# A row softmax in hardware loops: four slots and semaphores that count down, for six slots and a written-out order

## The chip, the cores and the metric

The kernel runs on one core of a Trainium2 chip. The metric is the device time of one execution in microseconds (us), lower being better. Ten executions of the kernel before gave a median of 318.81 us, between 318.66 and 319.29.

Five engines of the core run their own instruction streams [...]. Of them this kernel uses the vector engine (DVE), the scalar engine (ACT) and the sync engine (SP), which here only issues transfers. Transfers between the main memory (HBM) and the on-chip memory are carried by 16 DMA engines. SP's transfers stand in one queue and ACT's in another.

## What is computed

```python
def setup_inputs():
    batch, seq, dim = 32, 512, 1024
    return {"x": np.random.randn(batch, seq, dim).astype(np.float32), "temperature": 0.5}

def reference(x, temperature):
    scaled = x / temperature
    shifted = scaled - np.max(scaled, axis=-1, keepdims=True)
    exp_x = np.exp(shifted)
    return (exp_x / np.sum(exp_x, axis=-1, keepdims=True)).astype(np.float32)
```

There are 32 x 512 = 16,384 rows of 1,024 fp32 numbers, 67.1 MB to be read and as much to be written. The temperature is a constant of the program.

## The kernel before

The rows are cut into 16 blocks of 1,024. Each of the 128 partitions takes 8 rows of a block, which lie behind one another in HBM, 32 KB in all. So a block is one load of 4 MB, 128 runs of 32 KB, and one store of the same shape. On chip the blocks stand in a ring of 48 rows a partition (`RING = 48`), that is six places of 8 rows, used in turn. A block is loaded into its place, changed there and stored from there.

The work on a block is done in two groups of four rows (`GROUP = 4`). For a group, DVE takes the maximum of its four rows in one instruction (`maximum`, L91) and multiplies the four maxima by minus the scale (`shift`, L101). ACT computes one exponential for each row, with that number as bias, and sums the row on the way (`exponential`, L109; the sum is fetched by a second instruction for each row, the READ_ACCUMULATOR). DVE inverts the four sums (`invert`, L122) and multiplies each row by its own (`divide`, L128).

All of it stands in one critical section, in which the framework adds no waits and keeps the order as written; the kernel has its own semaphores. Every semaphore only counts up, and each wait names the total it waits for (`topped` at g + 1 and so on), so that the wait is carried by the instruction that needs it. The three streams are:

- SP (L142): the 16 loads in order. The first six are issued at once; from then on load i waits until the store of block i - 6 has landed. At the end SP waits for the stores that are still out (L158).
- ACT: for each group g of 32 the four exponentials, and after the exponentials of the first group of block i + 1 the store of block i (`store`, L149), which waits until DVE has divided all of block i.
- DVE: the loop quoted here. The division of a group comes after the maximum of the next group, and so the last group of a block is divided after the first maximum of the next block, which waits for that block's load.

```python
        for g in range(len(groups) + 1):
            if g < len(groups):
                maximum(g)
                shift(g)
            if g > 0:
                invert(g - 1)
                divide(g - 1)
```

Everything is written out: there is no loop in the program that the chip runs.

Of the kernel before, what the change touches and what calls it, by code (L numbers as in the profile page):

```python
# [1 line left out]

# [4 lines left out]

LOADS = [8] * 16  # L10

STORES = [[8]] * 16

RING = 48

GROUP = 4


def _places(loads, ring):
    places, p = [], 0  # L20
    for k in loads:
        if p + k > ring:
            p = 0
        places.append(p)
        p += k
    return places


@with_exitstack
def kernel(  # L30
    ctx: ExitStack,
    tc: tile.TileContext,
    x: bass.AP,
    temperature: bass.AP,
    out: bass.AP,
):
    nc = tc.nc
    f32 = mybir.dt.float32
    scale = 1.0 / float(temperature)
    extreme = mybir.AluOpType.max if scale > 0 else mybir.AluOpType.min  # L40

    P = 128
    xf = x.flatten_outer_dims()
    of = out.flatten_outer_dims()
    n, d = xf.shape
    assert sum(LOADS) * P == n

    places = _places(LOADS, RING)
    first = [sum(LOADS[:i]) for i in range(len(LOADS))]
    total = sum(LOADS)  # L50

    pool = ctx.enter_context(tc.tile_pool(name="data", bufs=1))
    ring = pool.tile([P, RING, d], f32, name="ring")
    top = pool.tile([P, total], f32, name="top")
    bias = pool.tile([P, total], f32, name="bias")
    sums = pool.tile([P, total], f32, name="sums")
    recip = pool.tile([P, total], f32, name="recip")


    parts = []  # L60
    for i, ks in enumerate(STORES):
        j = 0
        for k in ks:
            parts.append((i, places[i] + j, first[i] + j, k))
            j += k
        assert j == LOADS[i]

    groups, part_end = [], []
    for i, s, r, k in parts:
        for a in range(0, k, GROUP):  # L70
            groups.append((i, s + a, r + a, min(GROUP, k - a)))
        part_end.append(len(groups))

    loaded = [tc.alloc_semaphore(f"loaded{i}") for i in range(len(LOADS))]
    stored = [tc.alloc_semaphore(f"stored{i}") for i in range(len(parts))]
    topped, biased, summed, inverted, scaled = (
        tc.alloc_semaphore(name)
        for name in ("topped", "biased", "summed", "inverted", "scaled")
    )

    def dram(t, r, k, i):

        block = t[P * first[i] : P * (first[i] + LOADS[i]), :]
        block = block.rearrange("(p k) d -> p k d", p=P, k=LOADS[i])
        return block[:, r - first[i] : r - first[i] + k, :]

    def maximum(g):
        i, s, r, k = groups[g]
        if g == 0 or groups[g - 1][0] != i:
            nc.vector.wait_ge(loaded[i], 16)  # L90
        nc.vector.tensor_reduce(  # L91
            out=top[:, r : r + k],
            in_=ring[:, s : s + k, :],
            axis=mybir.AxisListType.X,
            op=extreme,
        ).then_inc(topped, 1)

    def shift(g):
        i, s, r, k = groups[g]
        nc.vector.wait_ge(topped, g + 1)  # L100
        nc.vector.tensor_scalar_mul(  # L101
            bias[:, r : r + k], in0=top[:, r : r + k], scalar1=-scale
        ).then_inc(biased, 1)

    def exponential(g):
        i, s, r, k = groups[g]
        nc.scalar.wait_ge(biased, g + 1)
        for a in range(k):
            ins = nc.scalar.activation(  # L109
                ring[:, s + a, :],  # L110
                ring[:, s + a, :],
                mybir.ActivationFunctionType.Exp,
                bias=bias[:, r + a : r + a + 1],
                scale=scale,
                accum_out=sums[:, r + a : r + a + 1],
            )
        ins.then_inc(summed, 1)

    def invert(g):
        i, s, r, k = groups[g]  # L120
        nc.vector.wait_ge(summed, g + 1)
        nc.vector.reciprocal(recip[:, r : r + k], sums[:, r : r + k]).then_inc(inverted, 1)  # L122

    def divide(g):
        i, s, r, k = groups[g]
        nc.vector.wait_ge(inverted, g + 1)
        for a in range(k):
            ins = nc.vector.tensor_scalar_mul(  # L128
                ring[:, s + a, :], in0=ring[:, s + a, :], scalar1=recip[:, r + a : r + a + 1]
            )  # L130
        ins.then_inc(scaled, 1)

    def load(i):
        nonlocal free_to
        s, r, k = places[i], first[i], LOADS[i]

        for n, (l, s1, r1, k1) in enumerate(parts):
            if l < i and s1 < s + k and s < s1 + k1 and n > free_to:
                for b in range(free_to + 1, n + 1):
                    nc.sync.wait_ge(stored[b], 16)  # L140
                free_to = n
        nc.sync.dma_start(out=ring[:, s : s + k, :], in_=dram(xf, r, k, i)).then_inc(  # L142
            loaded[i], 16
        )

    def store(n):
        l, s, r, k = parts[n]
        nc.scalar.wait_ge(scaled, part_end[n])
        nc.scalar.dma_start(out=dram(of, r, k, l), in_=ring[:, s : s + k, :]).then_inc(  # L149
            stored[n], 16  # L150
        )

    free_to = -1
    with tc.tile_critical():  # L154
        for i in range(len(LOADS)):
            load(i)
        for b in range(free_to + 1, len(parts)):
            nc.sync.wait_ge(stored[b], 16)  # L158


        for g in range(len(groups) + 1):
            if g < len(groups):
                exponential(g)
            for n in range(len(parts)):
                if part_end[n] == g:
                    store(n)


        for g in range(len(groups) + 1):
            if g < len(groups):  # L170
                maximum(g)
                shift(g)
            if g > 0:
                invert(g - 1)
                divide(g - 1)


# [1 line left out]
_INS = ['x', 'temperature']  # L179
_OUTS = [((32, 512, 1024), 'float32')]  # L180

_NUMBERS = {'temperature': 0.5}


# [26 lines left out]
```

## Time and profile before

| | us |
|---|---|
| median of ten executions | 318.81 |
| the profiled execution, its own time | 319.1 |
| its span, from the first to the last instruction | 317.3 |
| one maximum of four rows on DVE (L91), mean | 4.414 |
| one division of a row on DVE (L128), mean | 0.749 |
| one exponential of a row on ACT (L109), mean | 1.137 |
| median from issue to landing, load | 51.3 |
| median from issue to landing, store | 38.0 |

The span is what all positions below refer to; 0 is its start. The execution's own time is 1.8 us longer than the span. Durations of neighbouring instructions on one engine overlap a little: a division takes 0.749 us by itself, but four in a row take 2.74. "Landing" is the moment when a transfer's semaphore has received its last count.

### The profile page before, as it was taken

The numbers are of one execution on the slowest core, as the hardware profiler recorded it, in microseconds if no ns is written. First come the engines' busy times: TensorE is split into PE (matmuls) and PEld (weight loads), VectorE is DVE, ScalarE is ACT, GpSimd is POOL, SyncE is SP. The second block draws the span as 40 slices with busy tenths as digits, with TensorE's granted clock in tenths as the row PEclk, the third lists the DMA queues.
The fourth block names the chain that finished last, engine by engine and source line by source line (L and its number), as shares of the span: only waits on it lengthen the run. The fifth ranks groups of instructions, "written<-read, shape, count | busy, mean of one in ns | idle before, by whom it ended". The sixth has DMA issues, their size and how long they took to land.

```text
span 317.3 us, 568 instructions
## 1 busy us (share of the span) xinstructions
DVE 235.4 (74%) x224; ACT 149.6 (47%) x257; POOL 0.2 (0%) x4
## 2 busy tenths in 40 slices
DVE  0399999999689494995949869496793967949710
ACT  1076666666526255361554606455163551635500
POOL 0000000000000000000000000000000000000000
DMA  8999999999999999999999999999999999999994
GB/s 322 405 463 401 397 459 434 425 452 409 454 405 459 405 454 421 438 454 405 459 401 463 401 459 421 435 450 409 459 405 455 409 450 430 430 446 413 459 405 207
DMA packets 4612, 134.25 MB, mean 423 GB/s; under 512 B 512, under 2 KB 512, under 8 KB 512
## 3 DMA queue, kind: packets, MB, share of 16 engines
q1 hardware_dynamic: 2304, 67.11, 49.4%
q10 hardware_dynamic: 2304, 67.11, 49.0%
q14 instruction: 4, 0.03, 0.0%
HBM read 67.11 MB, written 67.11 MB: 423 GB/s over the span
## 4 chain that ended last, share of the span: by engine, by line
DVE 72%; another core or an unknown queue 16%; DMA 4%; ACT 3%; issue 1%; SPq 0%
DVE top L91 43%; DVE ring L128 27%; DMA ring<-in_x_dram 4%; ACT ring L109 3%; DVE bias L101 2%; DVE recip L122 1%; SPq L206 0%; SPq L154 0%
## 5 line engine op out<-in xcount | busy, mean ns | idle before, releaser
L109 ACT ACTIVATE ring<-ring,bias 128x1024 f32<-128x1024 f32 x128 | 145.4, 1137 | 149.4 <-DVE bias L101 149.4
L91 DVE TENSOR_REDUCE top<-ring 128x4 f32<-128x4096 f32 x32 | 141.3, 4414 | 63.2 <-DMA ring<-in_x_dram 63.2
L128 DVE TENSOR_SCALAR ring<-ring,recip 128x1024 f32<-128x1024 f32 x128 | 87.7, 749 | 1.1
L109 ACT ACTIVATION_READ_ACCUMULATOR ring<-ring,bias 128x1 f32 x128 | 23.9, 187 | 0.0
L122 DVE RECIPROCAL recip<-sums 128x4 f32<-128x4 f32 x32 | 5.5, 171 | 2.0 <-ACT ring L109 2.0
L101 DVE TENSOR_SCALAR bias<-top 128x4 f32<-128x4 f32 x32 | 5.4, 169 | 1.1
L109 ACT ACT_TABLE_LOAD x1 | 1.3, 1283 | 0.9 <-SPq L154 0.9
L192 POOL MEMSET const-bfloat16-1.0<- 128x1 bf16 x1 | 0.1, 101 | 0.0
L192 POOL MEMSET const-uint8-127<- 128x1 uint8 x1 | 0.1, 101 | 0.0
L192 POOL MEMSET const-float32-0.0<- 128x1 f32 x1 | 0.1, 98 | 0.2 <-issue 0.2
L192 POOL MEMSET const-float32-1.0<- 128x1 f32 x1 | 0.1, 98 | 0.0
## 6 DMA issues: line engine op xcount, KB each, us to landing
ring<-in_x_dram SPq DMA_DIRECT2D x16, 4096.0 KB, 51.3
out_dram<-ring ACTq DMA_DIRECT2D x16, 4096.0 KB, 38.0
```

What stands on the lines that cost most here:

```text
L91: nc.vector.tensor_reduce(out=top[:, r : r + k], in_=ring[:, s : s + k, :], axis=mybir.AxisListType.X, op=extreme,).then_inc(topped, 1)
L101: nc.vector.tensor_scalar_mul(bias[:, r : r + k], in0=top[:, r : r + k], scalar1=-scale).then_inc(biased, 1)
L109: ins = nc.scalar.activation(ring[:, s + a, :], ring[:, s + a, :], mybir.ActivationFunctionType.Exp, bias=bias[:, r + a : r + a + 1], scal ...
L122: nc.vector.reciprocal(recip[:, r : r + k], sums[:, r : r + k]).then_inc(inverted, 1)
L128: ins = nc.vector.tensor_scalar_mul(ring[:, s + a, :], in0=ring[:, s + a, :], scalar1=recip[:, r + a : r + a + 1])
L192: nc = _bacc.Bacc("TRN2", target_bir_lowering=False, num_devices=1)
```

## The change

The ring has four slots of 8 rows a partition in place of six. The 16 blocks are done in four turns of four; block 4t + s uses slot s. Rows are assigned to blocks and partitions as before, and every transfer is still 4 MB in 128 runs of 32 KB.

DVE and ACT each run a hardware loop over the four turns (`Fori`), whose body holds the work of four blocks written out. A loop body is the same in each turn, so its waits can't name a growing total. In its place `take` is used: an instruction that waits until the semaphore has reached a count and then takes that count off. The semaphores of the loads and between the engines work in this way; `stored` still counts up, since its only waits are on SP, which has no loop.

On DVE the order within a block is now both maxima with their shifts, then both inversions and divisions; a block is finished before the next is begun. On ACT a block's store follows the exponentials of the same block. Its address in HBM is worked out from the loop's counter.

The last slot's final store is waited for in a second critical section.

```diff
-LOADS = [8] * 16
+SLOTS = 4
-STORES = [[8]] * 16
+ROWS = 8
-RING = 48
 GROUP = 4
...
+    xv = xf.rearrange("(t s p k) d -> s p t (k d)", s=SLOTS, p=P, k=ROWS)
+    ov = of.rearrange("(t s p k) d -> s p t (k d)", s=SLOTS, p=P, k=ROWS)
...
-    ring = pool.tile([P, RING, d], f32, name="ring")
-    top = pool.tile([P, total], f32, name="top")
+    ring = pool.tile([P, SLOTS, ROWS, d], f32, name="ring")
+    top = pool.tile([P, ROWS], f32, name="top")
...
+    def take(engine, sem, count=1):
+        engine.wait_ge(sem, count).then_inc(sem, -count)
...
+    def maximum(s, a):
         nc.vector.tensor_reduce(
+            out=top[:, a : a + GROUP],
+            in_=ring[:, s, a : a + GROUP, :],
             axis=mybir.AxisListType.X,
             op=extreme,
         ).then_inc(topped, 1)
-        nc.vector.wait_ge(topped, g + 1)
+        take(nc.vector, topped)
         nc.vector.tensor_scalar_mul(
...
+    def exponential(s, a):
+        take(nc.scalar, biased)
+        for r in range(a, a + GROUP):
...
+    def divide(s, a):
+        take(nc.vector, summed)
+        nc.vector.reciprocal(recip[:, a : a + GROUP], sums[:, a : a + GROUP]).then_inc(
+            inverted, 1
+        )
+        take(nc.vector, inverted)
+        for r in range(a, a + GROUP):
+            ins = nc.vector.tensor_scalar_mul(
+                ring[:, s, r, :], in0=ring[:, s, r, :], scalar1=recip[:, r : r + 1]
+            )
+        if a == starts[-1]:
+            ins.then_inc(scaled, 1)
...
+    with tc.tile_critical():
+        for t in range(turns):
+            for s in range(SLOTS):
+                if t > 0:
+                    nc.sync.wait_ge(stored[s], 16 * t)
+                nc.sync.dma_start(
+                    out=ring[:, s].rearrange("p k d -> p (k d)"), in_=xv[s][:, t, :]
+                ).then_inc(loaded[s], 16)
+        for s in range(SLOTS - 1):
+            nc.sync.wait_ge(stored[s], 16 * turns)
+        with nc.vector.Fori(0, turns):
+            for s in range(SLOTS):
+                take(nc.vector, loaded[s], 16)
+                for a in starts:
+                    maximum(s, a)
+                for a in starts:
+                    divide(s, a)
+        with nc.scalar.Fori(0, turns) as t:
+            for s in range(SLOTS):
+                for a in starts:
+                    exponential(s, a)
+                take(nc.scalar, scaled)
+                nc.scalar.dma_start(
+                    out=ov[s][:, bass.ds(t, 1), :],
+                    in_=ring[:, s].rearrange("p k d -> p (k d)").unsqueeze(1),
+                ).then_inc(stored[s], 16)
+    with tc.tile_critical():
+        nc.sync.wait_ge(
+            stored[-1], 16 * turns, synchronizes=[nc.sync.lower_ap(ring[:, SLOTS - 1])]
+        )
```

More of the change, by code (lines that the diff above doesn't have):

```diff
@@ L6 @@
 from concourse._compat import with_exitstack
-LOADS = [8] * 16
-STORES = [[8]] * 16
-RING = 48
+SLOTS = 4
+ROWS = 8
 GROUP = 4
[L19 to L26, printed above, removed]
 @with_exitstack
@@ L45 @@
     n, d = xf.shape
[L46 to L50, printed above, removed]
+    turns = n // (P * ROWS * SLOTS)
+    assert turns * P * ROWS * SLOTS == n and ROWS % GROUP == 0
+    xv = xf.rearrange("(t s p k) d -> s p t (k d)", s=SLOTS, p=P, k=ROWS)
+    ov = of.rearrange("(t s p k) d -> s p t (k d)", s=SLOTS, p=P, k=ROWS)
     pool = ctx.enter_context(tc.tile_pool(name="data", bufs=1))
-    ring = pool.tile([P, RING, d], f32, name="ring")
-    top = pool.tile([P, total], f32, name="top")
[L55 to L75, printed above, removed]
+    ring = pool.tile([P, SLOTS, ROWS, d], f32, name="ring")
+    top = pool.tile([P, ROWS], f32, name="top")
+    bias = pool.tile([P, ROWS], f32, name="bias")
+    sums = pool.tile([P, ROWS], f32, name="sums")
+    recip = pool.tile([P, ROWS], f32, name="recip")
+    loaded = [tc.alloc_semaphore(f"loaded{s}") for s in range(SLOTS)]
+    stored = [tc.alloc_semaphore(f"stored{s}") for s in range(SLOTS)]
     topped, biased, summed, inverted, scaled = (
@@ L79 @@
     )
[L81 to L90, printed above, removed]
+    def take(engine, sem, count=1):
+        engine.wait_ge(sem, count).then_inc(sem, -count)
+    starts = range(0, ROWS, GROUP)
+    def maximum(s, a):
         nc.vector.tensor_reduce(
-            out=top[:, r : r + k],
-            in_=ring[:, s : s + k, :],
+            out=top[:, a : a + GROUP],
+            in_=ring[:, s, a : a + GROUP, :],
             axis=mybir.AxisListType.X,
@@ L96, in maximum @@
         ).then_inc(topped, 1)
-    def shift(g):
-        i, s, r, k = groups[g]
-        nc.vector.wait_ge(topped, g + 1)
+        take(nc.vector, topped)
         nc.vector.tensor_scalar_mul(
-            bias[:, r : r + k], in0=top[:, r : r + k], scalar1=-scale
+            bias[:, a : a + GROUP], in0=top[:, a : a + GROUP], scalar1=-scale
         ).then_inc(biased, 1)
[L105 to L108, printed above, removed]
+    def exponential(s, a):
+        take(nc.scalar, biased)
+        for r in range(a, a + GROUP):
@@ L109, in exponential @@
             ins = nc.scalar.activation(
-                ring[:, s + a, :],
-                ring[:, s + a, :],
+                ring[:, s, r, :],
+                ring[:, s, r, :],
                 mybir.ActivationFunctionType.Exp,
-                bias=bias[:, r + a : r + a + 1],
+                bias=bias[:, r : r + 1],
                 scale=scale,
-                accum_out=sums[:, r + a : r + a + 1],
+                accum_out=sums[:, r : r + 1],
             )
         ins.then_inc(summed, 1)
[L119 to L127, printed above, removed]
+    def divide(s, a):
[5 more added lines that the diff above has]
+        for r in range(a, a + GROUP):
             ins = nc.vector.tensor_scalar_mul(
-                ring[:, s + a, :], in0=ring[:, s + a, :], scalar1=recip[:, r + a : r + a + 1]
+                ring[:, s, r, :], in0=ring[:, s, r, :], scalar1=recip[:, r : r + 1]
@@ L130, in divide @@
             )
[L131 to L143, printed above, removed]
-        )
@@ L146, in store @@
[L146 to L175, printed above, removed]
+        if a == starts[-1]:
+            ins.then_inc(scaled, 1)
```

## The prediction

> **What bounds the kernel now.** The page first: its slices show the DMA engines at nine tenths or more from the first slice to the last but one, while DVE, the busiest engine, is at 74% of the span.
>
> ```profile
> span 317.3 us, 568 instructions
> DVE 235.4 (74%) x224; ACT 149.6 (47%) x257; POOL 0.2 (0%) x4
> DVE  0399999999689494995949869496793967949710
> DMA  8999999999999999999999999999999999999994
> ```
>
> Then the waits, DVE's and the SP queue's own. DVE is stopped by landing loads only (63.2 us), and SP may not issue the next load before a store has landed (224.5 us). ACT's 149.4 us behind DVE costs nothing, for ACT has little to do.
>
> ```profile
> ACT ring L109 <- DVE bias L101: 149.4, 31, 15.7
> DVE top L91 <- DMA ring<-in_x_dram: 63.2, 12, 13.2
> DVE recip L122 <- ACT ring L109: 2.0, 2, 1.8
> ```
> ```profile
> SPq L142 <- DMA out_dram<-ring: 224.5, 10, 52.2
> ```
>
> So it is a circle: store lands, load is issued, load lands, DVE works, store is issued. The busy time by stretches says who sets its pace (columns: length, busy DVE, ACT and POOL, clock, DMA share, GB/s).
>
> ```profile
> 105.00:244.00 139.00, 103.08 (x98) 64.94 (x112) 0.00 (x0) 1.00 1.00 433
> 244.00:283.00 39.00, 29.45 (x28) 18.56 (x32) 0.00 (x0) 1.00 1.01 435
> 283.00:303.00 20.00, 17.64 (x19) 9.28 (x16) 0.00 (x0) 1.00 1.01 434
> ```
>
> 433 to 435 GB/s at a DMA share of 1.0: one block (4.19 MB in, 4.19 MB out) takes 8.39 MB / 433 GB/s = 19.37 us, and SP issues loads at 212.09 and 231.44, 19.35 apart. DVE needs only 14.8 a block. The engines are busy to the end because in each ring several transfers stand in line, as the times to landing tell: one transfer alone needs 12.3 or 12.9, the median load 51.3 and store 38.0.
>
> ```profile
> DMA to landing us min/median/max: 12.9/38.0/39.4
> ```
>
> Last, one block's work on DVE and ACT at the start, which the change orders anew:
>
> ```profile
> 13.23 4.42 DVE L91 TENSOR_REDUCE top<-ring 128x4 f32<-128x4096 f32 x1 [13.23 <-DMA ring<-in_x_dram]
> 17.68 0.17 DVE L101 TENSOR_SCALAR bias<-top 128x4 f32<-128x4 f32 x1
> 17.76 4.41 DVE L91 TENSOR_REDUCE top<-ring 128x4 f32<-128x4096 f32 x1
> 17.89 1.15 ACT L109 ACTIVATE ring<-ring,bias 128x1024 f32<-128x1024 f32 x1 [15.71 <-DVE bias L101]
> ...
> 22.55 0.18 DVE L122 RECIPROCAL recip<-sums 128x4 f32<-128x4 f32 x1 [0.18 <-ACT ring L109]
> 22.77 2.74 DVE L128 TENSOR_SCALAR ring<-ring,recip 128x1024 f32<-128x1024 f32 x4
> ...
> 26.87 0.18 ACT L109 ACTIVATION_READ_ACCUMULATOR ring<-ring,bias 128x1 f32 x1
> ```
>
> [...] with loads alone, landings should be 4.19 MB / 433 GB/s = 9.69 apart, and 39.4 for a store is two turns of 19.4, with one store ahead of it and loads sharing. [...]
>
> **The change, part by part.**
>
> *DVE's order within a block.* Before, the second half of block i is divided after the first reduce of block i+1, so DVE never waits for ACT in the body. After, a block is finished before the next begins: max, max, divide, divide. From the rows above, counted from the block's start at 13.23: first exp at 4.66; eight activations end at 27.05 - 13.23 = 13.82; reciprocal 0.02 later, divisions 0.22 after that, 2.74 long; the next reduce may start 0.08 before they end (25.43 against 25.51 in the trace): 13.82 + 0.02 + 0.22 + 2.74 - 0.08 = 16.72 us a block, against 14.8. The difference is DVE waiting for ACT's second group.
>
> *The takes.* Each wait becomes an instruction of its own that waits and counts down. Not shown on DVE; SP's semaphore instructions took 17 to 28 ns. Lower bound 0.03, upper 0.3; I take 0.1. In a block's chain stand four or five (topped, biased, summed, inverted; the one on "loaded" is passed while the divisions run): 0.45. A DVE block is then C = 17.2 us, range 16.9 to 18.1. Queued behind DVE's wait for "summed" are the division and the next block's reduce; ACT's wait for "scaled" holds back the next block's exponentials, but those aren't due until 4.66 into that block.
>
> *Loop edges.* Three on each of DVE and ACT. DVE's body is 4 x 21 = 84 instructions, ACT's some 4 x 20 and address arithmetic: [...] beside the last divisions already queued (2.74). Zero taken; [...]
>
> *Stores with a register address.* Before 0.34 on ACT's queue. With register arithmetic and the take I take 0.5 in all from the last division to the issue, bounds 0.3 and 2.
>
> *Four slots for six.* This is what matters. A slot's turn is 4 x 19.37 = 77.5 us: C + issue 17.7, leaving 59.8 for load and store together. To keep the DMA engines full a load needs 19.4 (shared) + 2.6 (fixed: the first landed 12.27 after its issue, 9.69 of it data) = 22.0. So the body still stays DMA-bound: 16.72 to 18.1 is under 19.37. What gets thin is the line of stores at the end.
>
> I followed both rings transfer by transfer: each in order, 9.68 us alone, 19.36 when both have work, 1.4 from issue to the first byte and 1.16 from the last to the semaphore, slot loaded again when its store lands. For the kernel before this ledger gives the last load at 281.2 and the last store at 313.1; the trace has 283.23 and 315.8 (SP's last wait). The missing 2.0 and 2.7 are small delays at single transfers (a load interval of 20.08 for 19.36 near 76, for example), which I add to both. For the kernel after:
> - Loads 0 to 3 land at 13.2, 22.9, 32.5 and 51.0 (the fourth shares with store 0).
> - DVE works without a pause, block starts at 13.2, 30.4, 47.6, 64.8, 82.0, 99.2, 116.4, 133.6; stores issue 17.7 after each. Store 0 (30.9) lands at 51.9 and load 4 at 73.8, before its turn at 82.0. DMA idles nowhere.
> - From block 8 on each load lands later than DVE is ready: 151.2, 170.6, ... 19.35 apart, the last at 286.7. Stores take about 35.6, loads 24.5.
> - End: when the last load's last byte is in (285.5), 2.74 stores are unwritten. All but the last need 1.74 x 9.68 = 16.8 us; the last moves its first byte 1.16 + 17.7 + 1.4 = 20.3 us later. The DMA engines stand idle for the difference, 3.5 us, and the last store lands at 286.7 + 17.7 + 12.2 = 316.6.
>
> Before, this gap didn't exist: the last store was issued at 302.95 and the one ahead landed only at 315.8 - 9.65 = 306.2. So the loss is 316.6 - 313.1 = 3.5 us. DVE order alone would win (17.7 after the last load instead of 302.95 - 283.23 = 19.7), but the last load comes 5.5 later, since stores no longer lag.
>
> *Second critical section.* It waits for the last slot; its joins lie beside the last store (12 us). Zero, at most 0.3.
>
> Sum: 319.1 + 3.5 = 322.6 for an execution like the profiled one; on the median of the runs, 318.81 + 3.5 = 322.3, rounded to 322.2.
>
> **The rivals.**
> *A, not slower.* Loads get more than half of the rings' turns while both are full, so the last load lands 3 us or more earlier and 2.1 stores are left to hide the last block. For it: load 3 landed at 48.8 in the trace where my ledger says 49.0, and store 0 at 56.0 instead of 54.8. Against it: from there on the ledger's landings lie a steady 1 to 2 us before the trace's. It decides when the lag of stores at the last load reaches 20.3 us of work. Time 318.5 (same), down to 317.5 if some delays vanish with shorter lines.
> *B, DVE becomes the bound.* Last store at 13.2 + 16 C + 0.5 + 12.2 without pause; this overtakes the ledger at C = 18.2, that is takes at 0.33 or edges of 4 us with dear takes. At C = 18.8 the last landing is 326.7 (the small delays fall into pauses that DVE no longer has), + 3.0 to the median: 329.7.
> *C, edges or dynamic stores are dear but hidden in part.* Stores 2 us late give 317.9 in the ledger for 316.6, edges of 4 us 319.6: 323.5 and 325.2.
> *D, the transfers change.* [...] Against it: each row is one run of 32 KB in both kernels.
>
> **How the numbers follow.** Forecast (tail open, 320 to 323.4) 0.62; A 0.12; B 0.10; C 0.14; D 0.02. Time 322.2. About 0.2% (0.64 us) is what a measurement can tell from none. The range takes the forecast's own, half of A and all of C: 319.0 to 327.0. Faster 0.04, same 0.08, slower 0.88.
>
> **What would show it.** Right: DVE waits for loads only from about block 8 on; DVE idles about 1.7 us for ACT before each second reciprocal; 433 GB/s through the body; the last load lands at 288 to 289, and a slice below 400 GB/s stands just before the last store. Wrong: DVE never waiting for a load after the start (B), an edge visible as a gap every fourth block (C), or a last load before 286 (A).

## The result, and the profile after

| | before | after |
|---|---|---|
| median of the runs, us | 318.88 (30 runs, 318.66 to 319.46) | 321.44 (9 runs, 320.79 to 322.23) |
| profiled execution, own time | 319.1 | 321.12 |
| its span | 317.3 | 319.3 |

The changed kernel takes 1.008 times as long (95% interval 1.0072 to 1.0088), 2.56 us more. The forecast was 322.2, 3.3 us more.

The page of the changed kernel, its first lines and the DMA's rates:

```profile
span 319.3 us, 792 instructions
DVE 237.9 (74%) x224; ACT 153.0 (48%) x260; POOL 0.2 (0%) x4
DMA  8999999999999999999999999999999999999947
GB/s 328 398 456 427 382 439 447 406 445 410 447 435 423 443 419 443 435 423 447 415 443 435 427 443 415 447 431 431 443 415 447 431 431 443 415 443 435 431 209 328
```

The body is as full as before. What is new stands in the last two slices: a 4 and a 7, where the kernel before had a 9 and a 4, and 209 GB/s in the last but one. The busy time by stretches of the end shows it more closely, the changed kernel first, then the one before (length, busy DVE, ACT, POOL, clock, DMA share, GB/s):

```profile
298.00:304.00 6.00, 3.75 (x8) 5.55 (x10) 0.00 (x0) 1.00 0.90 388
304.00:308.00 4.00, 2.74 (x4) 0.00 (x0) 0.00 (x0) 1.00 0.31 131
308.00:318.00 10.00, 0.00 (x0) 0.00 (x0) 0.00 (x0) 1.00 0.86 367
```
```profile
298.00:304.00 6.00, 3.04 (x6) 1.94 (x4) 0.00 (x0) 1.00 1.01 437
304.00:308.00 4.00, 0.00 (x0) 0.00 (x0) 0.00 (x0) 1.00 0.94 401
308.00:316.00 8.00, 0.00 (x0) 0.00 (x0) 0.00 (x0) 1.00 0.64 274
```

Before, the share stays above 0.9 up to 308 us and falls only with the last transfer. After, it is 0.31 while DVE makes the last divisions, and then the engines carry one lone store. "Lone" means here that no other transfer is in line. The end on DVE and on ACT's queue, from the timeline of the changed kernel:

```profile
289.42 4.42 DVE L62 TENSOR_REDUCE top<-ring 128x4 f32<-128x4096 f32 x1 [1.90 <-DVEq L57]
...
303.70 0.18 DVE L88 RECIPROCAL recip<-sums 128x4 f32<-128x4 f32 x1 [1.57 <-DVEq L57]
304.03 2.74 DVE L93 TENSOR_SCALAR ring<-ring,recip 128x1024 f32<-128x1024 f32 x4
307.00 0.34 ACTq L123 DMA_DIRECT2D out_dram<-ring  x1
```

The last load landed at 289.28, the last store was issued 17.7 us later. By the trace's landing events the two stores ahead of it had landed at 295.85 and 305.51, and it landed at 318.10: 12.59 us behind its neighbour, where in a full line a store follows at 9.65.

One block early in the run, before loads set the pace, from the same timeline:

```profile
31.68 4.41 DVE L62 TENSOR_REDUCE top<-ring 128x4 f32<-128x4096 f32 x1
...
36.24 0.17 DVE L69 TENSOR_SCALAR bias<-top 128x4 f32<-128x4 f32 x1
36.31 4.41 DVE L62 TENSOR_REDUCE top<-ring 128x4 f32<-128x4096 f32 x1
36.53 1.15 ACT L76 ACTIVATE ring<-ring,bias 128x1024 f32<-128x1024 f32 x1 [7.98 <-ACTq L57]
...
41.31 0.18 DVE L88 RECIPROCAL recip<-sums 128x4 f32<-128x4 f32 x1 [0.27 <-DVEq L57]
...
45.95 0.18 DVE L88 RECIPROCAL recip<-sums 128x4 f32<-128x4 f32 x1 [1.57 <-DVEq L57]
46.28 2.74 DVE L93 TENSOR_SCALAR ring<-ring,recip 128x1024 f32<-128x1024 f32 x4 [0.15 <-DVEq L57]
48.94 4.41 DVE L62 TENSOR_REDUCE top<-ring 128x4 f32<-128x4096 f32 x1
```

A block takes 48.94 - 31.68 = 17.26 us. Line 57 is the take; DVE idles 1.57 before the second reciprocal, for ACT. One take in a chain costs 0.12, where the 0.1 of the forecast was a guess: from the reduce's end (31.68 + 4.41 = 36.09) to the shift 36.24 - 36.09 = 0.15, where the wait carried by the instruction cost 0.03 in the kernel before (13.23 + 4.42 = 17.65, shift at 17.68).

From the changed kernel, its waits (line, what it waited for: total, times, longest), then one of the page's groups (busy, mean ns | idle before), then DVE's instructions of the loop's line (ns min/median/max, first and last start):

```profile
DVE recip L88 <- DVEq L57: 34.1, 32, 1.6
DVE top L62 <- DVEq L57: 24.5, 8, 13.2
```
```profile
L76 ACT ACT_TABLE_LOAD x4 | 5.1, 1283 | 44.1 <-ACTq L57 44.1
```
```profile
L110 DVEq ALU_OP  x4: 40/40/52, 81.3 to 304.2; - x4
L110 DVEq COMPARE_BRANCH  x4: 50/62/69, 81.4 to 304.2; - x4
```

DVE's 63.2 us of waiting for loads have become 24.5 (13.2 of each are the first load), and 34.1 of waiting for ACT have come. A loop edge takes 0.1 us of DVE's queue (40 and 62 ns), while divisions already queued are running. One thing wasn't in the prediction at all: ACT loads its table in each turn, four times 1.28 us.

### The profile page after: what moved, and what is told of

Same layout as the page of the kernel before. It is cut to its first block, busy times and chain, and to the rows that moved or that the text cites. A ratio compares the mean times of both kernels' runs of the same rounds, so it can differ in the third digit from the quotient of the medians.

```text
span 319.3 us, 792 instructions
## 1 busy us (share of the span) xinstructions
DVE 237.9 (74%) x224; ACT 153.0 (48%) x260; POOL 0.2 (0%) x4
## 5 line engine op out<-in xcount | busy, mean ns | idle before, releaser
L62 DVE TENSOR_REDUCE top<-ring 128x4 f32<-128x4096 f32 x32 | 141.2, 4414 | 24.5 <-DVEq L57 24.5
L88 DVE RECIPROCAL recip<-sums 128x4 f32<-128x4 f32 x32 | 5.7, 178 | 34.1 <-DVEq L57 34.1
```

What stands on the lines that cost most here:

```text
L62: nc.vector.tensor_reduce(out=top[:, a : a + GROUP], in_=ring[:, s, a : a + GROUP, :], axis=mybir.AxisListType.X, op=extreme,).then_inc(to ...
L88: nc.vector.reciprocal(recip[:, a : a + GROUP], sums[:, a : a + GROUP]).then_inc(inverted, 1)
```

## The experiments

Times are medians; beside each, the ratio to the kernel before on the same chip. From the trace's packet records I worked out two sums for each kernel. One is the excess: what the 32 KB packets took beyond 1.206 us each, divided by 16 engines. 1.206 us is the pace of a full line, in which an engine carries its eight packets of a transfer in 9.65 us; a single undisturbed packet is on record with 1.213, so only differences of the excess tell something (a half-size packet of e5 counts with 0.603). The other is the engines' mean idle time between 285 us and the last packet.

| | us | ratio, 95% interval | excess | idle at the end |
|---|---|---|---|---|
| before | 318.88 | | 3.3 | 1.8 |
| after | 321.44 | 1.008 (1.0072 to 1.0088) | 3.8 | 3.7 |
| e1: four slots | 324.33 | 1.0174 (1.016 to 1.0188) | 3.4 | 7.0 |
| e2: order by blocks | 323.89 | 1.0177 (1.0154 to 1.02) | 6.6 | 2.6 |
| e3: both, no loops | 323.36 | 1.0136 (1.012 to 1.0151) | 3.8 | 5.6 |
| e4: after, ACT written out | 321.81 | 1.0092 (1.0078 to 1.0106) | 4.1 | 3.9 |
| e5: after, last store halved | 318.36 | 0.9989 (0.9977 to 1.0) | 3.8 | 0.9 |
| e6: after, DVE busier | 328.46 | 1.0298 (1.0283 to 1.0313) | 4.6 | 7.6 |
| e7: e3, later start | 321.65 | 1.0082 (1.0069 to 1.0095) | 3.5 | 3.9 |
| e8: e2, later start | 318.94 | 1.0004 (0.9995 to 1.0012) | 3.5 | 1.3 |

For the change itself the idle end grows by 1.9 and the excess by 0.4 us; the last packet comes 317.76 - 315.45 = 2.3 us later. In every run the two sums, and in e6 its later start, account for the end of the last packet to about 0.1 us.

**e1, four slots alone.**

```diff
-RING = 48
+RING = 32
```

> The kernel before with RING 32 for 48: four slots, nothing else. My theory (the loss is the time the DMA engines stand idle before the last store; which slot count and order let the stores lag decides it): the ledger, with the lone store's fixed time corrected to the 1.45 us that the changed kernel shows, gives a last landing 4.4 us later than before, so about 323.3 us, more than the changed kernel's 321.4, because a block's last division still waits for the next load. Rival 'the loops cost it': no change, 318.9. Rival 'the slot count alone is the change's 2.6 us': 321.4.

Measured 324.33, 5.5 us more than before: slots alone cost more than the whole change, as expected, and 1 us more than the ledger had. In the order of before, a block's store waits for the next block's load; with four slots the last two stores both go out alone (landings 296.25, 308.89 and 321.06, so 12.6 and 12.2 apart). The busy time of e1 by stretches:

```profile
280.00:300.00 20.00, 15.39 (x15) 9.51 (x18) 0.00 (x0) 1.00 0.80 346
300.00:312.00 12.00, 7.97 (x12) 4.64 (x8) 0.00 (x0) 1.00 0.71 306
```

**e2, the order alone.** A block's store stands behind its own exponentials, and the blocks are written one by one:

```diff
-                if part_end[n] == g:
+                if part_end[n] == g + 1:
                     store(n)
...
-        for g in range(len(groups) + 1):
-            if g < len(groups):
-                maximum(g)
-                shift(g)
-            if g > 0:
-                invert(g - 1)
-                divide(g - 1)
+        for n in range(len(parts)):
+            block = range(part_end[n] - 2, part_end[n])
+            for g in block:
+                maximum(g)
+                shift(g)
+            for g in block:
+                invert(g)
+                divide(g)
```

> The kernel before with six slots and no loop, but each block finished before the next begins (max, max, divide, divide; the block's store right behind its own exponentials). Theory: stores of earlier blocks still cover the last block, the ledger's last landing is unchanged, 318.9 within 0.4. Rival 'DVE's waiting for ACT inside a block costs time': 16 times some 2 us of DVE idle would give up to 30 us more, 348; even a tenth of it would show as 322.

Missed: 323.89. But DVE still waits for loads in the body (37.9 us in all), so it has time to spare there, and the rival, DVE's idle time, isn't the cause either. The packets show another one. After the first 60 us, 48 of 1,472 load packets took over 1.5 us, against 3 in the kernel before; most stand in knots once a block (at 171, 191, 211, 231 and 250 us), where a store begins some 2.4 us after a load. Loads landed only 2.4 us ahead of stores (171.0 and 173.4; before, 166.1 and 173.3). Here the body itself is slower, and e8 tests why.

**e3, slots and order, no loops.** e2 with `RING = 32`.

> Four slots and the order by blocks together, without loops, takes or register addresses. Theory: ledger +0.8 us on the kernel before, 319.7; the loop's instructions (17.25 us a block for 16.75, a later store issue, a table load in each turn) then account for the remaining 1.6 to 1.8 us of the changed kernel. Rival 'the loops cost nothing, the slots all': 321.4. Rival 'the loops cost all': 318.9.

Missed too: 323.36, slower than the changed kernel, which does the same with more instructions. Neither rival fits. The idle end is 5.6 us, for the last load landed at 292.2 (289.3 in the changed kernel). The gap had arisen in the second turn: load 4 landed at 78.2 here and at 75.3 there, and afterwards both kernels keep 19.36 us a block, except for one load in each that came 1.0 us late. The stretch near the end:

```profile
300.00:312.00 12.00, 7.19 (x12) 6.06 (x12) 0.00 (x0) 1.00 0.54 229
```

**e4, ACT's loop written out.**

```diff
-        with nc.scalar.Fori(0, turns) as t:
+        for t in range(turns):
...
-                    out=ov[s][:, bass.ds(t, 1), :],
+                    out=ov[s][:, t : t + 1, :],
```

> The changed kernel with ACT's loop written out (its takes stay; DVE's loop stays): no table load in turns 2 to 4, no register address, no edge on ACT. Theory: the table loads lie before the last block or in DVE's pause for a load, and the ledger gives only 0.2 us less than the changed kernel: 321.2. Rival 'ACT's table loads are on the path': three of 1.28 us less, 317.6.

321.81: nothing is gained, so the three further table loads, the register address and ACT's edges are off the path. The rival's 317.6 is out. The first table load stays where it was, behind the first maximum, and it is the only one left:

```profile
L76 ACT ACT_TABLE_LOAD x1 | 1.3, 1283 | 18.2 <-ACTq L57 18.2
```

**e5, the last store in two halves.** `scaled` is raised after each four rows; ACT's last turn is written out, and for the last block:

```diff
+            for a in starts:
+                take(nc.scalar, scaled)
+                nc.scalar.dma_start(
+                    out=ov[s][:, turns - 1, a * d : (a + GROUP) * d],
+                    in_=ring[:, s, a : a + GROUP].rearrange("p k d -> p (k d)"),
+                ).then_inc(stored[s], 16)
```

> The changed kernel with its last store in two halves, the first issued as soon as the first four rows of the last block are divided (ACT's last turn written out, for the loop can't tell it apart; its other three turns stay a loop). Theory (DMA engines idle before the last store): the first half, issued some 13 us after the last load, stands in line behind the store before; the last half needs 4.84 us in place of 9.68 after 307.0, so the last landing moves from 318.1 to 315.2: 318.6 us, the kernel before's time. Rival 'the loss lies in the body' (slower blocks, edges): no gain, 321.4.

318.36 for the 318.6 expected: the change's whole loss is gone, and the only transfer that differs is the last block's. (Writing out ACT's last turn gains nothing by itself, as e4 shows for all four; the body runs at 433 GB/s, as in the changed kernel.) The halves were issued at 302.87 and 307.51, the first while the store before was under way, and the busy time by stretches shows the gap closed:

```profile
300.00:312.00 12.00, 5.66 (x9) 4.20 (x8) 0.00 (x0) 1.00 1.00 426
```

The same stretch in the changed kernel:

```profile
300.00:312.00 12.00, 5.04 (x9) 3.56 (x8) 0.00 (x0) 1.00 0.73 311
```

Its median is the lowest of all, 0.1% under the kernel before, but the interval reaches 1, so the two can't be told apart.

**e6, DVE busier.** Behind each block's divisions:

```diff
+                nc.vector.tensor_scalar_mul(copy[:], in0=idle[:], scalar1=2.0)
```

The extra work is on a tile of its own that is filled once ahead of the loop, which puts the first packet off from 1.9 to 4.3 us.

> The changed kernel with one more DVE instruction of about 1.4 us at the end of each block, behind its last division (it computes on a tile of its own; the block's store doesn't wait for it). Theory: a DVE block of 17.25 us has about 0.9 us of room before DVE sets the pace; with 1.37 more the ledger gives 11 us on the changed kernel, 332.4, and DVE waits for no load after the first. Rival 'DMA-bound with room to spare': 321.4. Rival 'DVE is on the path already': 16 x 1.37 = 21.9 more, 343.

328.46, less the 2.4 us of the later start 326.1: 4.6 more than the changed kernel. The 332.4 expected was missed, by 6.3 us without the later start. The larger part of that is the instruction, which took only 1.13 us of DVE's time a block for the 1.37 expected: 16 x 0.24 = 3.8. Its waits show the new bound:

```profile
DVE top L65 <- DVEq L60: 12.6, 1, 12.6
```

Only the first load is waited for. DVE's blocks follow at (296.69 - 15.55) / 15 = 18.74 us on average, table loads included. In the changed kernel the same average is (289.42 - 13.25) / 15 = 18.41, set by the last load, while DVE alone would need 17.26 and the 1.2 of a table load in every fourth block, 17.56. So there were 0.85 us of room a block, and 15 x (18.74 - 18.41) = 5.0 us had to come out at the last block; 4.6 did in the whole time. Both rivals are out.

**e7, e3 starting later.** One reading of the first two rows by DVE before the first maximum:

```diff
+            if n == 0:
+                nc.vector.wait_ge(loaded[0], 16)
+                nc.vector.tensor_scalar_mul(copy[:], in0=ring[:, :2, :], scalar1=2.0)
```

> Four slots and the order by blocks without loops (as e3), with one DVE instruction of 1.4 us put before the first block's maximum; nothing else. The account so far: the looped kernel was faster than e3 (321.4 to 323.4) because its first block takes 1.2 us longer, the first stores come later, the loads of the second turn get ahead and more stores are left to cover the end. Then a later start makes it faster: last load at 290 to 291 for 292.2, time about 322. Rival 'a delay is a delay': 324.8. Rival 'the gap between e3 and the changed kernel has another cause': 323.4.

321.65: 1.15 us of added work at the start made the kernel 1.7 us faster. Load 4 landed at 76.4 instead of 78.2, the last load at 290.2 instead of 292.2, and the idle end shrank from 5.6 to 3.9 us:

```profile
300.00:312.00 12.00, 5.42 (x9) 4.04 (x8) 0.00 (x0) 1.00 0.73 311
```

So how far loads are ahead of stores is settled in the first turns and kept. The looped kernel has such a delay built in: its first exponential waits for the table, 1.28 us from 18.10 on, which e3 loads at 0.9 us, while the first block is still on its way.

**e8, e2 starting later.** The first maximum is computed twice (4.4 us):

```diff
+                nc.vector.tensor_reduce(
+                    out=bias[:, 0:4], in_=ring[:, 0:4, :],
+                    axis=mybir.AxisListType.X, op=extreme,
+                ).then_inc(early, 1)
+                nc.vector.wait_ge(early, 1)
```

> Six slots and the order by blocks (as e2), with the first block's first maximum computed twice (4.4 us more before the first block). In e2 load packets took 1.5 to 2.0 us for 1.2 in each block, where a load's and a store's first packets ran side by side (landings of a load and the next store 2.4 us apart; 7.2 in the kernel before). Account: the two start in step, and that slows the load's packets. The delay moves the stores out of step by some 9 us for good: the slow packets go, and the kernel gets faster by about 4 us in spite of the delay, 319 to 320. Rival 'the order itself costs': 323.9 or, with the delay added, 328.

318.94, the time of before. Landings of a load and the next store lie some 11 us apart now (164.2 and 175.5), and 2 of 1,440 load packets took over 1.5 us. The body by stretches, e2 first, then e8:

```profile
100.00:280.00 180.00, 140.60 (x132) 87.65 (x153) 0.00 (x0) 1.00 1.00 426
```
```profile
100.00:280.00 180.00, 150.19 (x143) 91.68 (x160) 0.00 (x0) 1.00 1.00 433
```

So the order by blocks costs nothing by itself with six slots: the same order is slow or not with the phase of its transfers, that is, with how far behind a load a store begins, and the slow packets come and go with it. Why transfers that started 2.4 us apart slowed each other in e2, no run tells.

## Why the prediction was right

**The body.** Forecast: still DMA-bound at a full share, blocks of 17.2 us on DVE, waits for loads from block 8 on, 1.7 us of waiting for ACT in each block, no cost of edges. Shown: 433 GB/s from 100 to 280 us, 17.26, waits from block 9 on, 1.57 us, edges of 0.1 us under queued work.

```profile
100.00:280.00 180.00, 145.51 (x135) 90.86 (x155) 0.00 (x0) 1.00 1.00 433
```

That 19.37 us a block would stay the DMA's pace was an estimate from the 433 GB/s of before; the eight kernels read from 100 to 280 us moved 426 (e2) to 434 GB/s (before, e1, e7).

e6 found the room of DVE at 0.85 us a block, near the 1.0 between 17.2 and the 18.2 named as rival B's threshold.

**The end.** Forecast: the last load at 288 to 289, 3.5 us of idle engines, a slice below 400. Shown: 289.28, just outside, 12.59 - 9.65 = 2.9 us by the landings, a slice of 209. e5 shows the place: closing that gap gave back 3.1 us.

**The sizes.** The ledger with its 2.7 us of delays puts the last landing at 319.3; it came at 318.10. The last load was 0.6 late. The last store took 11.1 us from issue to landing for the 12.2 that I had taken from the first load: a lone store's fixed time is 11.10 - 9.65 = 1.45 us, not 2.6. (e1, e3 and e7 end with a lone store too, and it took 11.1 in each.) The ledger's split of the 2.6, 1.4 ahead of the first byte and 1.16 behind the last, was an estimate: the changed kernel's last store began its first packet 0.84 us after the issue, and its last packet ended 0.35 before the landing. And no further 0.7 us of delay came after the last load. 0.6 - 1.1 - 0.7 = -1.2. So the term that was mis-sized most is the lone store's latency. A slip stands beside it: 318.81 + 3.5 is 322.3, and 322.2 was set down.

**What was not seen.** The table loads cost nothing in e4's comparison, and they delayed the first block in a way that helped, as e7 shows for such a delay.

**What the reasoning had too simple.** The ledger treats both rings as evenly shared, which held on average (from 105 to 244 us loads began 0.496 of the packets before and 0.504 after), and all engines as equal. It met the changed kernel, but gave 319.7 for e3 (323.36) and no change for e2 (323.89). For e3, with its shorter blocks, it even has the wrong direction: less loss than in the changed kernel, where there was more. In e3 it misses how the second turn's loads fall behind, for e2 it has no price for a store that begins 2.4 us after a load. So part of the agreement is luck: the changed kernel suffered from neither. How the 3 us of e3's load 4 arise, packet by packet, stays open; that a shift of the start moves them is shown, the reason isn't. One difference is on record: store 2 is issued at 66.94 us in the changed kernel and at 63.60 in e3, and from 68 to 70 us the changed kernel's engines carry load 4 alone, while in e3 stores take 0.44 of their time. It can't be all of it, for in e7 stores take 0.40 there and load 4 still lands 1.8 us earlier than in e3.

**The rivals.** A (not slower) would have needed the last load 3 us earlier; it came at 289.28. B is not reached, by e6. C has no support: ACT's edges, the table loads and the stores' register address are off the path by e4, and DVE's edges by the trace alone (0.1 us under queued work; the 4 us an edge were an estimate, and no edge in the trace takes that long). D is out, since the changed kernel's data still go in 4,096 packets of 32 KB, as before.

## What to carry to other kernels

When the DMA engines bound the body, as here (433 GB/s at a share of 1.0), ask what the buffers keep in line at the end: two slots fewer cost e1 5.5 us, and its engines' idle end grew from 1.8 to 7.0. Count the stores still out when the last load lands, against the time from that load to the last store's issue. If they don't cover it, try cutting the last store first: here it brought the time back to that of the kernel with six slots. And before a reordering is blamed or praised for a per cent, shift its start by a few microseconds: here the phase of loads against stores, set in the first turns, moved the times by 1.7 us (e3, e7) and 5 us (e2, e8).

## What the runs showed of the hardware

- Where a store began 2.4 us after a load in each block, the two slowed: 426 GB/s for 433 over 180 us, 48 load packets of over 1.5 us for 2 or 3. A delay of 4.4 us at the start put 11 us between them, removed it and made the kernel 5 us faster (e2, e8).
- A lone 4 MB store landed 11.1 us after its issue; the first load, with others in line behind it, took 12.2 to 12.3. No run has a load that is truly alone.
- A hardware loop on ACT loaded the table of its activation function in each of four turns (1.28 us each); the written-out stream loaded it once.
- A separate wait-and-count-down instruction on DVE cost 0.12 us in a dependent chain, though it ran for 21 ns itself (changed kernel, L57).
- The written-out kernels fetch instructions on the way (8 KB packets at 240.8 us before, 247.8 in e1, 247.3 in e3); the load then under way landed 0.9 to 1.0 us late in all three. The looped kernel has no such fetch so late (its two are at 64.1 and 67.9 us), and its loads keep to 19.36 us from 115 us on. That the fetch is the cause is not shown, and two records speak against it: a fetch at 198.6 us in the kernel before made no load late, and one at 232.0 in e8 goes with a load only 0.1 us late.
